# Nine transposes of constants put ahead of three FFN products, and the sum of the second gate moved to the FFN's end

## The chip, the cores and the metric

The kernel runs on one core of a Trainium2 chip. The metric is the device time of one execution in microseconds (us), lower being better; where runs of a kernel differ, their median counts.

## What is computed

One decoder block on a sequence of 256 tokens with 1024 channels, batch 1, in float32:

```python
mod = (jax.nn.silu(c) @ w_ada[l] + b_ada[l]).astype(x.dtype)
sh1, sc1, gt1, sh2, sc2, gt2 = jnp.split(mod[:, None, :], 6, axis=-1)
h = rmsnorm(x, g_mix[l]) * (1.0 + sc1) + sh1
proj = h @ w_in[l]
...
x = x + gt1 * (mixed @ w_out[l])

h = rmsnorm(x, g_ffn[l]) * (1.0 + sc2) + sh2
up = causal_dwconv(h @ w_up[l], ffn_conv_w[l], ffn_conv_b[l])
val, gte = jnp.split(up, 2, axis=-1)
x = x + gt2 * ((jax.nn.silu(gte) * val) @ w_down[l])
```

`w_up` has 2 x 2816 columns and `w_down` 2816 rows, so that the FFN holds most of the work. `gt2`, the second gate, is used only where the FFN's result is added to `x`.

## The kernel before

Channels lie on the 128 partitions and the 256 tokens along the free dimension. Every weight is cut into pieces of 128 x 1024 floats. A piece is loaded by SP's queue into a ring of eight buffers (`raw`, two pieces in a buffer), and split into two tiles of the reduced float32 type of TensorE (PE): `hi`, a rounded copy that ScalarE (ACT) makes at L166, and `lo`, the rest, which VectorE (DVE) makes at L171. The activations are split in the same way (`hhi`, `hlo`; `ahi`, `alo`). A product of 128 x 128 weights with 128 x 256 activations is then three matmuls, `mm3` at L204: hi with hi, hi with the activations' lo, lo with hi. Each loads its own 128 x 128 weights, so that PE runs a chain of pairs of a weight load and a matmul of 256 columns.

The order of every engine's work is the order in which the code is written; no scheduler moves anything. The FFN is a list of 66 steps, `FFN_SEQ`, numbered n from 0: three value and gate pairs ("v", "g") first, and then "d", "v", "g" in turn, "d" being the product with one block of `w_down`. Steps 0 to 2 run together, and the last two in `finish`. A step is 24 matmuls: eight times `mm3`, over the channels for "v" and "g" (into the tiles `pu` and `pg`), over the eight blocks of output channels for "d" (into `pod`). `up_psum` takes the PSUM tile of a step: `pu` from a pool of two banks that other tiles share, `pg` from two banks in turn. After the product of a "v" or "g" step ACT (L758) and DVE (L764) make the convolution out of the PSUM tile.

The second gate is the product of `silu(c)` with one section of `w_ada`. DVE adds it up in `gacc` in eight parts (`gate_part`, L569), at the ends of steps 10, 13 and so on to 31. `gate_rows` (L577) then adds over the partitions with four matmuls of ones, each of 32 by 256 (eight instructions in the trace), into a tile `psg` of the pool of `pu`; `mod_cols` (L600, L608) transposes that on DVE and adds the bias. The first user of the result is `residual` (L695), after the last step but two.

In the first third of the kernel, the attention, PE also transposes probabilities: three transposes of 128 x 128 (`pst`, L503) stand between the two halves of a product (`pb`, `pu` or `pc` there), eight times in all.

Of the kernel before, what the change touches and what calls it, by code (L numbers as in the profile page):

```python
# [14 lines left out]
P = 128  # L15
S = 256
# [34 lines left out]
GROUPS = [(0,), (1,), (2, 3), (4, 5), (6, 7)]  # L51
GATE_STEP = range(1, 9)
ADA_FFN = {(3, i): 10 + 6 * i for i in range(4)}
REP = 16
AHEAD = 2

# [2 lines left out]
def decoder_block(ctx: ExitStack, tc, xT_in, pp, ada1, ada2, wqkv, wst, out):  # L59
# [6 lines left out]
    ACT, DVE, PE, POOL = nc.scalar, nc.vector, nc.tensor, nc.gpsimd  # L66
# [14 lines left out]
    def pw(name):  # L81
        return psw.tile([P, 512], F32, tag="w", name=name)

    def p1(tag, name):
        return ps1.tile([P, 512], F32, tag=tag, name=name)
# [21 lines left out]
    need += [(NS + 2 * c - AHEAD - 0.5, ("w", NS // 2 + c)) for c in range(len(FFN_SEQ) // 2)]  # L107
    need += [(NS + st, ("a2",) + k) for k, st in ADA_FFN.items()]
    order += [k for _, k in sorted(need)]
# [30 lines left out]
    ident = cp.tile([P, P], F32, name="ident")  # L140
    make_identity(nc, ident)
    ones = cp.tile([P, P], F32, name="ones")
# [43 lines left out]
    def hi_to(i):  # L186

        while made["hi"] <= min(i, len(PIECES) - 1):
            k = made["hi"]
            WH[k] = split_hi(piece(k))  # L190
            made["hi"] += 1

    def lo_to(i):

        while made["lo"] <= min(i, len(PIECES) - 1):
            k = made["lo"]
            W[k] = WH[k], split_lo(piece(k), WH[k])
            if k % 2:
                free(("w", k // 2))
            made["lo"] += 1  # L200

    def mm3(o, l, r, start, stop, shared=False, passes=(0, 1, 2)):

        for p in passes:  # L204
            PE.matmul(o, l[p == 2], r[p == 1], start=start and p == 0, stop=stop and p == 2, skip_group_check=shared)  # L205
# [4 lines left out]
    def cut(pair, i, w=P):  # L210
        return tuple(t[:, i * w:(i + 1) * w] for t in pair)


    def add_squares(ss, s2, first, last):

        for t in range(2):
            PE.matmul(ss[:, t * REP:(t + 1) * REP], s2[:, t * P:(t + 1) * P], ones[:, 0:REP], start=(first and t == 0), stop=last,  # L217
                      skip_group_check=True)

    def rms_root(ss, n, name):  # L220
        ms = wk.tile([P, 2], F32, tag="ms", name=f"ms_{name}")
        DVE.tensor_scalar(ms, ss[:, 0:2 * REP].rearrange("p (t n) -> p t n", n=REP)[:, :, 0], 1.0 / n, EPS, op0=OP.mult, op1=OP.add)
        r = wk.tile([P, 2], F32, tag="r", name=f"r_{name}")
# [337 lines left out]
    def gate_part(s, kk):  # L561

        i, k = divmod(kk, 2)
        a = ring["a2", s, i][:, k * D:(k + 1) * D]
        if kk == 0:
            gacc[s] = cp.tile([P, D], F32, tag="gacc", name=f"gacc{s}")
            DVE.tensor_scalar(gacc[s], a, cs[:, 0:1], None, op0=OP.mult)
        else:
            DVE.scalar_tensor_tensor(gacc[s], a, cs[:, kk:kk + 1], gacc[s], op0=OP.mult, op1=OP.add)  # L569
        if k == 1:  # L570
            free(("a2", s, i))
# [3 lines left out]
    def gate_rows(s, ps):  # L575
        for j in range(4):
            PE.matmul(ps[32 * j:32 * j + 32, 0:256], ones[:, 0:32], gacc[s][:, j * 256:(j + 1) * 256],  # L577
                      start=True, stop=True)
        sacc[s] = ps
# [17 lines left out]
    def mod_cols(s):  # L597

        tr = wk.tile([P, 256], F32, tag="tr", name=f"trm{s}")
        DVE.transpose(tr, sacc[s][:, 0:256])  # L600
        v = tr.rearrange("p (k q) -> p k q", q=32)[:, :, 0]
        b = par[:, PC["b_ada"] + 8 * (2 + s):PC["b_ada"] + 8 * (3 + s)]
        if s == 2:
            DVE.tensor_tensor(mod2[:, 0, :], v, bsc1[:, 1, :], op=OP.add)
            DVE.tensor_mul(mod2[:, 0, :], mod2[:, 0, :], par[:, PC["g_ffn"]:PC["g_ffn"] + KT])
        else:
            dst = {0: gate[:, 0, :], 1: mod2[:, 1, :], 3: gate[:, 1, :]}[s]
            DVE.tensor_tensor(dst, v, b, op=OP.add)  # L608
# [18 lines left out]
    for s in range(NS - 2):  # L627

        j, i = divmod(s, 3)
# [117 lines left out]
    PU, Y, ACTV = {}, {}, {}  # L747
    hall = [both(hT, slice(None), kt, slice(None)) for kt in range(KT)]

    def up_psum(n):  # L750
        w, j = FFN_SEQ[n]
        PU[w, j] = pw(f"pu{j}") if w == "v" else p1("vz"[j % 2], f"pg{j}")
        return PU[w, j][:, 0:S]
# [52 lines left out]
    def after_up(n, w, j):  # L806

        after(n + 1, conv_first, w, j, first=True)
        after(n + 1, conv_rest, w, j)
        if w == "g":  # L810
            after(n + 1, act_silu, j)
            after(n + 2, act_mul, j)
            after(n + 3 if j < NJ - 1 else n + 2, act_lo, j)

    def down(n, b, last, ds=None, ps=None):
        j = FFN_SEQ[n][1]
        for d in ds or (2 * b, 2 * b + 1):
            o = pd[b][:, (d % 2) * S:(d % 2 + 1) * S] if ps is None else ps[:, 0:S]
            mm3(o, cut(W[NS + n], d), ACTV[j], (j == 0 and d % 2 == 0) if ps is None else n == nl - 2, last,
                shared=True)  # L820
# [3 lines left out]
    nl = len(FFN_SEQ)  # L824
    for n in range(3, nl):
        w, j = FFN_SEQ[n]
        for f, a in early.pop(n, ()):
            f(*a)
        lo_to(NS + n + AHEAD - 1)
        hi_to(NS + n + AHEAD)  # L830
        for f, a in later.pop(n, ()):
            f(*a)
        if w != "d":
            ps = up_psum(n)
            for kt in range(KT):
                mm3(ps, cut(W[NS + n], kt), hall[kt], kt == 0, kt == KT - 1)
            after_up(n, w, j)
        elif n < nl - 2:
            for b in range(4):
                down(n, b, b == 3 and n == nl - 3)  # L840

        for (_, i), st in ADA_FFN.items():
            if n in (st, st + 3):
                gate_part(3, 2 * i + (n > st))
        end = max(ADA_FFN.values())
        if n == end + 5:
            gate_rows(3, pw("psg3"))
        if n == end + 6:
            mod_cols(3)


# [97 lines left out]
```

## Time and profile before

| | us |
|---|---|
| median of three timed runs | 338.1 |
| the three runs | 334.89, 338.10, 338.63 |
| the profiled execution's own time | 336.0 |
| its span, first to last instruction | 334.2 |

The profile is of one further execution, of which the span leaves out 1.8 us. The times of single instructions come from that execution; the duration of a matmul in it is modelled and overlaps the next one, so that the distance from one matmul's start to the next one's is the number to read.

### The profile page before, as it was taken

How to read it: one execution, taken by the hardware profiler on the slowest of the kernel's cores; microseconds unless marked ns; L12 is line 12 of the kernel's file. 1: busy time of each engine (PE TensorE's matmuls, PEld its weight loads, DVE VectorE, ACT ScalarE, POOL GpSimd, SP SyncE). 2: the span in 40 equal slices, each digit the busy share in tenths (PEclk: the TensorE clock that was granted, in tenths of full speed). 3: DMA queues.
4: the chain of work that ended last, by engine and by line, in shares of the span. 5: the costliest groups of instructions: out<-in, count | busy, mean ns of one | idle time of the engine just before them, and what ended most of it. 6: DMA issues, size and time to landing. Idle time of an engine off the chain costs nothing.

```text
span 334.2 us, 7175 instructions
## 1 busy us (share of the span) xinstructions
PE 325.1 (97%) x2996; PEld 310.1 (93%) x2996; DVE 250.1 (75%) x434; ACT 191.1 (57%) x334; POOL 18.9 (6%) x32
## 2 busy tenths in 40 slices
PE   8999999999999999999999999999999999999992
PEld 8988999888889998899999999999999999999991
DVE  3546774898976897699778888888777777777763
ACT  4334556888873475468655555555455555555460
POOL 1000000010131203000000000000000000000040
PEclk9999999999999999999999999999999999999997
DMA  7999999988996856635567675858464551000003
GB/s 268 419 419 421 411 418 421 358 324 348 358 372 273 310 187 258 227 152 178 202 222 281 218 286 196 297 190 324 151 230 156 224 177 78 0 2 0 2 0 126
DMA packets 12559, 79.23 MB, mean 237 GB/s; under 512 B 1392, under 2 KB 1520, under 8 KB 3952
## 3 DMA queue, kind: packets, MB, share of 16 engines
q1 hardware_dynamic: 12528, 78.79, 61.7%
q8 instruction: 23, 0.38, 0.4%
q14 instruction: 8, 0.07, 0.1%
HBM read 77.74 MB, written 1.05 MB: 236 GB/s over the span
## 4 chain that ended last, share of the span: by engine, by line
issue 56%; PE 33%; DMA 6%; DVE 1%; POOL 1%; SPq 1%; ACT 0%; DVEq 0%
DMA raw<-in_wqkv 6%; PE pox L205 6%; PE pq L205 5%; PE pc L205 4%; PE pb L205 4%; PE pu L205 3%; PE psm L589 2%; PE warm L205 1%; PE pv L205 1%; PE pss L217 1%; PE psr L269 1%; POOL sqr L704 1%; PE pss L471 1%; PE pso L517 1%; PE pst L503 1%
## 5 line engine op out<-in xcount | busy, mean ns | idle before, releaser
L171 DVE TENSOR_TENSOR lo<-raw,hi 128x1024 fp32r<-128x1024 f32 x86 | 104.6, 1222 | 4.9 <-ACT hi L166 4.8
L166 ACT CAST hi<-raw 128x1024 fp32r<-128x1024 f32 x86 | 88.9, 1041 | 2.1 <-PE pox L205 2.1
L205 PE MATMUL pu<-hhi,hi 128*128 128x256 f32 x208 | 58.5, 281 | 0.0
L205 PE MATMUL pu<-hhi,lo 128*128 128x256 f32 x208 | 57.8, 278 | 0.0
L205 PE MATMUL pu<-hlo,hi 128*128 128x256 f32 x208 | 57.7, 278 | 0.0
L205 PE MATMUL pg<-hlo,hi 128*128 128x256 f32 x176 | 49.0, 278 | 0.0
L205 PE MATMUL pg<-hhi,hi 128*128 128x256 f32 x176 | 48.9, 278 | 0.0
L205 PE MATMUL pg<-hhi,lo 128*128 128x256 f32 x176 | 48.9, 278 | 0.0
L205 PE MATMUL pod<-alo,hi 128*128 128x256 f32 x172 | 47.9, 279 | 0.0
L205 PE MATMUL pod<-ahi,lo 128*128 128x256 f32 x172 | 47.7, 278 | 0.0
L205 PE MATMUL pod<-ahi,hi 128*128 128x256 f32 x172 | 47.7, 278 | 0.0
L205 PEld LDWEIGHTS pu<-hhi,hi 128*128 128x128 f32 x208 | 39.1, 188 | 1.4 <-issue 0.7
L205 PEld LDWEIGHTS pu<-hlo,hi 128*128 128x128 f32 x208 | 39.1, 188 | 0.0
L205 PEld LDWEIGHTS pu<-hhi,lo 128*128 128x128 f32 x208 | 39.0, 187 | 0.0
L764 DVE SCALAR_TENSOR_TENSOR fyv<-pu,parf,fyv 128x255 f32<-128x255 f32 (+1 forms) x44 | 21.2, 482 | 20.0 <-ACT fyv L758 19.2
L758 ACT ACTIVATE fyv<-pu,parf 128x256 f32<-128x256 f32 x22 | 12.4, 564 | 39.8 <-PE pu L205 39.8
L205 PEld LDWEIGHTS pg<-hhi,hi 128*128 128x128 f32 x176 | 33.1, 188 | 0.0
L205 PEld LDWEIGHTS pg<-hlo,hi 128*128 128x128 f32 x176 | 33.0, 188 | 0.0
L205 PEld LDWEIGHTS pg<-hhi,lo 128*128 128x128 f32 x176 | 33.0, 187 | 0.0
L205 PEld LDWEIGHTS pod<-alo,hi 128*128 128x128 f32 x172 | 32.3, 188 | 0.1
L205 PEld LDWEIGHTS pod<-ahi,hi 128*128 128x128 f32 x172 | 32.3, 188 | 0.0
L205 PEld LDWEIGHTS pod<-ahi,lo 128*128 128x128 f32 x172 | 32.2, 187 | 0.0
(164 smaller groups left out, 652.2 us busy)
## 6 DMA issues: line engine op xcount, KB each, us to landing
raw<-in_wst SPq DMA_DIRECT2D x43, 1024.0 KB, 4.9
raw<-in_ada SPq DMA_DIRECT2D x24, 1024.0 KB, 8.3
raw<-in_wqkv SPq DMA_DIRECT2D x6, 768.0 KB, 14.6
raw<-in_wqkv SPq DMA_DIRECT2D x4, 256.0 KB, 7.0
out<-xp SPq DMA_DIRECT2D x4, 256.0 KB, 2.8
xp<-in_x SPq DMA_DIRECT2D x3, 256.0 KB, 3.9
raw<-in_wqkv SPq DMA_DIRECT2D x1, 512.0 KB, 9.6
xp<-in_x SPq DMA_DIRECT2D x1, 308.0 KB, 2.7
```

What stands on the lines that cost most here:

```text
L166: ACT.copy(hi[:, 0:n], raw)
L171: DVE.tensor_sub(lo[:, 0:n], raw, hi[:, 0:n].bitcast(F32))
L205: PE.matmul(o, l[p == 2], r[p == 1], start=start and p == 0, stop=stop and p == 2, skip_group_check=shared)
L217: PE.matmul(ss[:, t * REP:(t + 1) * REP], s2[:, t * P:(t + 1) * P], ones[:, 0:REP], start=(first and t == 0), stop=last, skip_group_check= ...
L269: PE.matmul(AR[g][32 * j:32 * j + 32, :], crep[:, k, :], a[:, k % (KT // n), j, :], start=(k == 0), stop=(k == KT - 1))
L471: PE.matmul(AT["s", h][:, c], qT[o:o + DH, p, q], kT[o:o + DH, p, k], start=True, stop=True)
L503: PE.transpose(ps[:, i * P:(i + 1) * P], AT["p", h][0][:, i * P:(i + 1) * P], ident)
L517: PE.matmul(ps[o:o + DH, c], vs[:, i, h * DH:(h + 1) * DH], AT["pt", h][:, k], start=(i == 0), stop=(i == 1))
L589: PE.matmul(sacc[s][32 * j:32 * j + 32, 0:256], crep[:, kk, :], a[:, k, j * 256:(j + 1) * 256], start=(kk == 0), stop=(kk == KT - 1))
L704: POOL.tensor_tensor(s2[:, d, :], s2[:, d, :], s2[:, e, :], op=OP.add)
L758: ACT.activation(Y[w, j], PU[w, j][:, 0:S], AF.Identity, bias=col("ffn_b", f), scale=col("ffn_w", 2 * 2 * NJ + f))
L764: DVE.scalar_tensor_tensor(y[:, d:], ps[:, 0:S - d], col("ffn_w", k * 2 * NJ + f), y[:, d:], op0=OP.mult, op1=OP.add)
```

## The change

Ahead of the products of steps 4, 7 and 10 (`TURNS`; "v" steps all three) PE makes three transposes of the constant tile `ones` into columns 256 to 383 of the step's own PSUM tile, columns that nothing reads. `gate_rows` for the second gate goes from the end of step 33 to the end of step 61, and `mod_cols` from 34 to 62. The eight parts of the sum on DVE stay where they are, as do all loads.

```diff
+TURNS = (4, 7, 10)
...
         if w != "d":
             ps = up_psum(n)
+            if n in TURNS:
+
+                for _ in range(3):
+                    PE.transpose(PU[w, j][:, S:S + P], ones, ident)
             for kt in range(KT):
                 mm3(ps, cut(W[NS + n], kt), hall[kt], kt == 0, kt == KT - 1)
...
-        end = max(ADA_FFN.values())
-        if n == end + 5:
+        if n == nl - 5:
             gate_rows(3, pw("psg3"))
-        if n == end + 6:
+        if n == nl - 4:
             mod_cols(3)
```

PE at the start of step 4 (`pu`), after the last matmuls of step 3 (`pg`); before:

```order
L205 MATMUL pg_1998<-hhi,hi 128x256
L205 MATMUL pg_1998<-hlo,hi 128x256
L205 MATMUL pg_1998<-hhi,lo 128x256
L205 MATMUL pu_2039<-hhi,hi 128x256
L205 MATMUL pu_2039<-hlo,hi 128x256
```

and with the change:

```order
L206 MATMUL pg_1998<-hhi,hi 128x256
L206 MATMUL pg_1998<-hlo,hi 128x256
L206 MATMUL pg_1998<-hhi,lo 128x256
L839 MATMUL pu_2039<-ident,ones 128x128 x3
L206 MATMUL pu_2039<-hhi,hi 128x256
L206 MATMUL pu_2039<-hlo,hi 128x256
```

Three transposes now stand between the two chains of matmuls; the same happens ahead of steps 7 and 10.

PE at the sum of the second gate, which before stands between step 33 (`pod`) and step 34 (`pu`):

```order
L205 MATMUL pod_1979<-ahi_2896,hi 128x256
L205 MATMUL pod_1979<-alo_2930,hi 128x256
L205 MATMUL pod_1979<-ahi_2896,lo 128x256
L577 MATMUL psg_3102<-gacc_2280,ones 32x256 x4
L205 MATMUL pu_3117<-hhi,hi 128x256
```

and with the change between step 61 (`pu`) and step 62 (`pg`):

```order
L206 MATMUL pu_4053<-hhi,hi 128x256
L206 MATMUL pu_4053<-hlo,hi 128x256
L206 MATMUL pu_4053<-hhi,lo 128x256
L578 MATMUL psg_4078<-gacc_2289,ones 32x256 x4
L206 MATMUL pg_4093<-hhi,hi 128x256
```

From step 11 to step 61 nothing but the chain of `mm3` is left on PE.

DVE where the gate's transpose now stands, with the change: behind the convolution of step 61 (`fyv`) and ahead of the `lo` of a later piece; the first user of the gate is in the last row.

```order
L765 SCALAR_TENSOR_TENSOR fyv_4083<-pu_4053,parf,fyv_4083 128x254
L601 STREAM_TRANSPOSE trm_4118<-psg_4078 128x256
L609 TENSOR_TENSOR gate<-trm_4118,xp 128x8
L172 TENSOR_TENSOR lo<-raw,hi 128x1024
L765 SCALAR_TENSOR_TENSOR fyg_4121<-pg_4093,parf,fyg_4121 128x255
L765 SCALAR_TENSOR_TENSOR fyg_4121<-pg_4093,parf,fyg_4121 128x254
L172 TENSOR_TENSOR lo<-raw,hi 128x1024
L774 TENSOR_TENSOR a_4157<-sg_4129,fyv_4083 128x256
L782 TENSOR_TENSOR alo_4161<-a_4157,ahi_4159 128x256
L696 SCALAR_TENSOR_TENSOR xp<-pod_1979,gate,xp 128x256 x2
```

Two instructions came in here, and left their place after step 33.

## Rows read from the trace of the kernel before

**Rows 1.** The page: busy time of PE, and the granted clock in 40 slices.

```profile
PE 325.1 (97%) x2996; PEld 310.1 (93%) x2996; DVE 250.1 (75%) x434; ACT 191.1 (57%) x334; POOL 18.9 (6%) x32
...
PEclk9999999999999999999999999999999999999997
```

**Rows 2.** Chain of waits in order of time, from the FFN's start: start us, us, what.

```profile
135.70 184.61 issue
```

**Rows 3.** Waits of PE in the whole span: us in total, times, longest us.

```profile
PE warm L159 <- POOL mhalf L145: 1.5, 1, 1.5
PE psr L269 <- DMA raw<-in_ada: 0.6, 1, 0.6
PE pss L217 <- POOL sqr L704: 0.5, 2, 0.3
```

**Rows 4.** Windows of nine steps: length, busy PE, PEld, DVE, ACT, POOL, clock, DMA.

```profile
149.24:174.68 25.44, 25.44 (x218) 25.44 (x217) 21.85 (x35) 17.24 (x27) 0.00 (x0) 1.00 0.56 200
...
200.12:225.56 25.44, 25.44 (x218) 25.44 (x217) 21.76 (x31) 14.32 (x22) 0.00 (x0) 1.00 0.62 224
242.97:267.45 24.48, 24.48 (x218) 24.48 (x217) 18.44 (x28) 14.35 (x22) 0.00 (x0) 1.00 0.55 200
...
291.93:316.41 24.48, 24.48 (x218) 24.48 (x217) 18.43 (x28) 13.93 (x21) 0.00 (x0) 1.00 0.01 1
```

**Rows 5.** Timeline of PE around the second gate's sum: start us, us, instruction.

```profile
233.92 0.28 PE L205 MATMUL pod<-ahi,lo 128*128 128x256 f32 x1
234.13 0.64 PE L577 MATMUL psg<-gacc,ones 128*32 128x256 f32 x8
234.70 0.39 PE L205 MATMUL pu<-hhi,hi 128*128 128x256 f32 x1
234.92 0.28 PE L205 MATMUL pu<-hlo,hi 128*128 128x256 f32 x1
235.04 0.28 PE L205 MATMUL pu<-hhi,lo 128*128 128x256 f32 x1
```

**Rows 6.** Chain of waits: twelve matmuls behind a group of three transposes.

```profile
65.32 1.42 PE pb L205 x12
...
69.53 1.37 PE pu L205 x12
```

**Rows 7.** Timeline of PE around one group of three transposes.

```profile
68.92 0.28 PE L205 MATMUL pu<-hhi,lo 128*128 128x256 f32 x1
69.04 0.49 PE L503 MATMUL pst<-ident,pr 128*128 128x128 f32 x3
69.28 0.36 PE L205 MATMUL pu<-hhi,hi 128*128 128x256 f32 x1
69.48 0.28 PE L205 MATMUL pu<-hlo,hi 128*128 128x256 f32 x1
```

**Rows 8.** Timeline of PE behind the first gate's sum: second and twelfth matmul.

```profile
100.25 0.28 PE L205 MATMUL pc<-hlo,hi 128*128 128x256 f32 x1
...
101.43 0.28 PE L205 MATMUL pc<-hhi,lo 128*128 128x256 f32 x1
```

**Rows 9.** Timelines of PE and of DVE: around step 31, and the FFN's end.

```profile
225.80 0.28 PE L205 MATMUL pu<-hhi,lo 128*128 128x256 f32 x1
...
221.64 1.23 DVE L171 TENSOR_TENSOR lo<-raw,hi 128x1024 fp32r<-128x1024 f32 x1
...
225.95 1.28 DVE L569 SCALAR_TENSOR_TENSOR gacc<-raw,cs,gacc 128x1024 f32<-128x1024 f32 x1
...
311.77 1.00 DVE L764 SCALAR_TENSOR_TENSOR fyv<-pu,parf,fyv 128x255 f32<-128x255 f32 x2 [1.39 <-ACT fyv L758]
...
317.81 0.87 DVE L695 SCALAR_TENSOR_TENSOR xp<-pod,gate,xp 128x256 f32<-128x256 f32 x2
```

**Rows 10.** Timeline of DVE: the second gate's transpose and bias.

```profile
234.84 0.45 DVE L600 STREAM_TRANSPOSE trm<-psg 128x256 f32<-128x256 f32 x1 [0.33 <-PE psg L577]
235.32 0.17 DVE L608 TENSOR_TENSOR gate<-trm,xp 128x8 f32<-128x8 f32 x1
```

## Prediction

> **What bounds the kernel now.** I read the page first: PE is busy for 97% of the span, at full granted clock until the last slice [rows 1]. Then the chain of waits in order of time: from 135.70 us on it shows 184.61 us in which nothing that the profile knows of is waited for, up to the norm at the end, 320.3 us [rows 2]. The list of PE's own waits is short, 2.6 us in the whole span, and none of it is in the FFN's steps [rows 3]. So the FFN is bound by the pace at which PE goes through its pairs of weight load and matmul, and a time can change there only through the number of instructions or through that pace.
>
> The pace is therefore the next thing to look at, in windows of nine equal steps, 216 matmuls each (the counts beside them take in one or two at the edges). Two windows ahead of the second gate's sum last 25.44 us, two behind it 24.48 us, at the same granted clock of 1.00 [rows 4]. The edges are starts of steps, chosen so that each window holds nine whole ones. That is 2.827 and 2.720 us a step, or 117.8 and 113.3 ns a matmul, for instructions of the same form. The load on the other engines doesn't explain it: DMA is at 0.55 in a fast window and 0.56 in a slow one. The timeline of PE shows where it turns: at the second gate's sum. Its eight short matmuls start at 234.13, the chain begins again at 234.70, and from its second matmul at 234.92 on the distances are 113 or 114 ns [rows 5]. PE thus has two paces, keeps the one that it has while the chain is unbroken (816 matmuls before, 768 behind, as I count them in the timeline), and takes one anew when the chain begins again after another kind of instruction. The change is about just that: it breaks the chain three times early, and takes away the break at which it turned.
>
> How often does a break end fast? Transposes of the same size stand eight times inside products of the attention. In the chain of waits the twelve matmuls behind three of these groups take 1.37 us, behind the other five 1.42 [rows 6], of which one of each stands there; the shorter ones are at the distance of 113 ns from the second matmul on. Behind breaks of other kinds the chain is nearly always slow: from the second to the twelfth matmul behind the first gate's sum it is 1.18 us in ten distances, 118 ns [rows 8]. The same sum, the second time, ended fast. I take the outcome for a matter of a few nanoseconds at the restart, and so for one that can differ from execution to execution.
>
> **The change part by part.** I sum against the profiled execution, 336.0 us.
>
> The transposes. From the start of the last matmul ahead of a group to that of the second behind it, 68.92 to 69.48, it is 0.56 us [rows 7]; two distances of 0.118 would be 0.235. A group costs 0.325, and three cost +0.98 us. Nothing hides that, since PE is the bound. Nobody else is held up: the products start 0.3 us later, and what feeds and empties them only gains by that. The transposes read constants, and the PSUM bank was already emptied for the product that follows.
>
> The pace from step 10 on. If the last group leaves PE fast, steps 10 to 33, 24 of them, take 0.107 us less each [rows 4]: -2.56. If it was already fast from step 7 or 4, it is 0.32 or 0.64 more; I take the middle, -0.32. If it stays slow, these steps cost nothing more than now, but steps 34 to 61, which are now fast, lose 28 x 0.107 = 3.0.
>
> A faster pace needs its feeding. DVE is the busiest other engine, with 21.76 of 25.44 us while the gate's parts are added up [rows 4]; the same work in 24.48 us would be 89%. The `lo` of step 31 is ready at 222.87, and first read at 225.80 [rows 9], 2.9 us ahead. A window of the FFN with gate parts, run fast, still leaves DVE free for 2.7 us, so I take no wait there. If a wait did come, it would also break the chain and draw a pace anew.
>
> The sum of gate 2. From the last matmul ahead, 233.92, to the second behind, 234.92, it is 1.00 us [rows 5], 0.765 more than two distances, and it costs that at either place. What it does to the pace of the four steps behind it is open: 0 to 4 x 0.107 = 0.43. I take +0.43, since most breaks of other kinds end slow. On DVE the transpose and the bias, 0.45 and 0.17 us [rows 10], now stand behind the convolution that ends at 312.77, and the gate is first used at 317.81 [rows 9]: 4.4 us of room with everything added, so nothing there. The `pl` tiles of the end take the two shared banks after the convolution and this transpose have read them, which is as early. Cover gone, it would cost at most 0.6.
>
> The sum for the fast case: 336.0 + 0.98 - 2.56 - 0.32 + 0.43 = 334.5; between 334.2 (fast from step 4) and 334.9 (from step 10), and 0.4 less where the gate's sum ends fast.
>
> To the timed runs. Three runs of one program at 334.89, 338.10 and 338.63 fit the same idea: an execution that stays slow throughout would be the profiled one plus 32 steps of 0.107, 339.4; two runs lie 0.8 to 1.3 below that, and the third 1.1 below the profiled one. So I read the lowest as a run that turned and the other two as runs that didn't, and the timed executions as 1.1 us shorter than the profile makes them. Then the fast case is 334.5 - 1.1 = 333.4, against a median of 338.1 that is itself of the slow kind. Without that shift it would be 334.5.
>
> [...]
>
> **The rivals.** First: the last group leaves PE slow. For it: five of eight groups in the attention did. Then the chain is slow up to step 61, where before it turned at step 34 in the profiled execution: 336.0 + 0.98 + 3.0 + 0.43 = 340.4, and with the shift 339.3. That is slower than before, by 1.2 us against the median. It decides at the third group alone if each group draws anew, whatever the first two did; if a fast chain stays fast through three transposes, one success in three suffices, with 1 - (5/8)^3 = 0.76 at the rate of [rows 6] against 0.38. No row shows a group that was entered fast; that is the largest unknown.
>
> Second: the pace has nothing to do with the breaks and changed at 234 us for another reason, say a load elsewhere. Against it: the last of DVE's gate parts ends at 227.23 [rows 9], and the chain stayed slow until the sum, 7 us later. Then the transposes are only a cost, 338.1 + 1.0 = 339.1.
>
> [...]
>
> Last, something of the move itself hurts: DVE late, or a break that leaves a worse pattern. More than 3 us of it would be needed.
>
> **How the numbers follow.** A measurement of this kernel tells a change of 1% from none, here 3.4 us, or a time under 334.7. Fast: 0.55, halfway between drawing anew and keeping, 0.38 and 0.76, with 333.4 and a range of its own of 332.9 to 334.9. Slow: 0.33, 339.3. Cost alone: 0.07, 339.1. Worse: 0.05, over 341.5. The fast case is faster by over 1% but for its upper end, so faster gets 0.53, same 0.41, slower 0.06. The range must hold both main cases, 332.9 to 339.5.
>
> **What would show it.** In the changed kernel's trace, windows of nine steps between 11 and 61 should all last 24.48 us; 25.44 is the first rival. Each group of transposes should add 0.32 us, and steps 4 to 10 show which one turned the pace. Behind the gate's sum, four steps tell whether it is lost. PE's waits should be as before. The prediction is wrong if the third group leaves PE slow in most executions, or if a fast chain meets waits on DVE.

## The result, and the profile after

The changed kernel takes 338.98 us, the kernel before 337.62 (medians of 20 runs each): a ratio of 1.0052, with a 95% interval of 1.0029 to 1.0076. It is slower by half a per cent, where 333.4 was forecast; the first rival had 339.3. Three of the 20 runs of the kernel before lie at 334.3 to 335.8 and the others at 337.2 or more; of the changed kernel none lies under 337.57. The times of several kernels here fall into two such groups, and an interval can leave out runs far above a kernel's fastest, so that medians are of all runs and the number of runs in the lower group stands beside them.

The profiled execution took 339.06 us, its span is 337.2. The chain of waits, from the FFN's start (start us, us, what):

```profile
135.41 188.69 issue
324.10 1.48 POOL sqr L705 x2
...
328.39 1.27 PE warm L160 x10
```

The stretch without a wait is 4.08 us longer than in [rows 2]. The list of PE's waits has the same three entries as [rows 3], none in the FFN. So the FFN is again the pace of PE and nothing else. Windows from the first group's start to the second's and on to the third's, then two of nine steps (length, busy PE, PEld, DVE, ACT, POOL, clock, DMA):

```profile
148.96:157.77 8.81, 8.81 (x77) 8.81 (x76) 8.67 (x16) 7.36 (x13) 0.00 (x0) 1.00 0.50 176
157.77:166.58 8.81, 8.81 (x77) 8.81 (x76) 6.46 (x10) 5.11 (x8) 0.00 (x0) 1.00 0.61 227
...
174.80:200.24 25.44, 25.44 (x218) 25.44 (x217) 21.77 (x31) 14.31 (x23) 0.00 (x0) 1.00 0.72 273
...
268.00:293.44 25.44, 25.44 (x219) 25.44 (x218) 18.42 (x28) 14.31 (x22) 0.00 (x0) 1.00 0.23 84
```

The first two hold a group (0.33 us, below) and 72 matmuls at 118 ns each, so they are slow. The last two are 25.44 us long, the slow windows of [rows 4]; the second of them lies where the kernel before, in its profile, had 24.48. All three groups left the chain slow, and it is slow to the end. Around the second group, in the timeline of PE:

```profile
157.65 0.28 PE L206 MATMUL pod<-ahi,lo 128*128 128x256 f32 x1
157.77 0.49 PE L839 MATMUL pu<-ident,ones 128*128 128x128 f32 x3
158.02 0.36 PE L206 MATMUL pu<-hhi,hi 128*128 128x256 f32 x1
158.22 0.28 PE L206 MATMUL pu<-hlo,hi 128*128 128x256 f32 x1
```

It is 0.57 us from the last matmul ahead to the second behind (0.56 in [rows 7]): a group costs 0.33, and three cost 0.99. The sum of gate 2 in its new place:

```profile
313.78 0.28 PE L206 MATMUL pu<-hhi,lo 128*128 128x256 f32 x1
313.99 0.64 PE L578 MATMUL psg<-gacc,ones 128*32 128x256 f32 x8
314.55 0.39 PE L206 MATMUL pg<-hhi,hi 128*128 128x256 f32 x1
314.78 0.28 PE L206 MATMUL pg<-hlo,hi 128*128 128x256 f32 x1
```

That is 1.00 us, as at [rows 5]. On DVE the transpose and the bias stand at 315.61 and 316.08, and the gate is first used at 321.60; nothing waits for them. And the groups of the attention, from the chain of waits:

```profile
65.04 1.42 PE pb L206 x12
...
69.25 1.37 PE pu L206 x12
...
83.73 1.36 PE pu L206 x12
...
87.89 1.36 PE pc L206 x12
```

The three stretches of 1.36 and 1.37 us stand at the same places of eight as in the profile before, of which [rows 6] shows one. That should not be so if each group were a draw.

### The profile page after: what moved, and what is told of

Read it like the earlier page. It is cut to its first block, busy times and chain, and to the rows that moved or that the text cites. A ratio compares the mean times of both kernels' runs of the same rounds, so it can differ in the third digit from the quotient of the medians.

```text
span 337.2 us, 7190 instructions
## 1 busy us (share of the span) xinstructions
PE 327.8 (97%) x3005; PEld 312.7 (93%) x3005; DVE 250.0 (74%) x434; ACT 190.9 (57%) x334; POOL 18.9 (6%) x32
## 4 chain that ended last, share of the span: by engine, by line
issue 56%; PE 34%; DMA 6%; POOL 1%; DVE 1%; SPq 0%; ACT 0%; DVEq 0%
PE pox L206 6%; PE pq L206 6%; DMA raw<-in_ada 6%; PE pc L206 4%; PE pb L206 4%; PE pu L206 3%; PE psm L590 2%; PE warm L206 1%; PE pv L206 1%; PE psr L270 1%; PE pss L218 1%; POOL sqr L705 1%; PE pss L472 1%; PE pso L518 1%; PE pst L504 1%
```

## The experiments

In the texts below a chain of matmuls is fast at 113 and slow at 118 ns; a group is a row of transposes ahead of a product. Transposes and added matmuls write columns that nothing reads. Edits are against the changed kernel unless another is named; a row of dots marks lines left out. Theory A says that what a break leaves is fixed by what stands there, B that moving the sum is what costs, C that every break draws anew.

**The two parts apart.** First the late sum alone, against the kernel before:

```diff
-        end = max(ADA_FFN.values())
-        if n == end + 5:
+        if n == nl - 5:
...
-        if n == end + 6:
+        if n == nl - 4:
```

> The sum of gate 2 at step 61, no transposes. Theory A (what ends a break slow or fast is fixed by what stands there, the transposes end slow, and most executions of the kernel before never turned at its sum either): about the kernel before's usual time, 337.6, and 1.0 us under the changed kernel's 338.98; all FFN steps up to 61 at 2.827 us. Theory B (the kernel before usually turns fast at step 33, and moving the sum is what costs): 28 x 0.107 = 3.0 us over the kernel before, and about the changed kernel's time or more.

337.84 us in 10 runs (337.25 to 339.60), against 336.86 before: ratio 1.004, interval 1.0003 to 1.0078. The chain is slow from the FFN's start to step 61. The lower group is gone: 9 of the 19 runs before in this comparison lie under 335.5, none of these does. Its distance to the changed kernel, 1.14 between the medians of two comparisons, is near the 0.99 of three groups. Then the transposes alone:

```diff
-        if n == nl - 5:
+        end = max(ADA_FFN.values())
+        if n == end + 5:
...
-        if n == nl - 4:
+        if n == end + 6:
```

> The three groups of transposes, the sum of gate 2 at step 33 as before. Theory A: 1.0 us over the kernel before in the usual execution, 338.6; the steps behind each group at 2.827 us; behind the sum fast in few executions, so that the profile probably shows slow ones there. Theory B: fast behind the sum, 1.0 us over the kernel before and 3 us under the changed kernel.

338.11 us (334.61 to 340.35, four of ten under 336.5), ratio 1.0017, 0.9966 to 1.0068. In the profile the first group left the chain fast and the second made it slow again, in windows of 72 matmuls each:

```profile
149.60:157.85 8.25, 8.25 (x75) 8.25 (x74) 8.14 (x15) 6.81 (x12) 0.00 (x0) 1.00 0.52 180
158.09:166.66 8.57, 8.57 (x75) 8.57 (x74) 6.53 (x10) 5.18 (x8) 0.00 (x0) 1.00 0.57 224
```

A group can thus undo the one before it. The lower times are back with the sum at 33, while with the same three groups and the late sum none of 20 runs had them. So the sum at 33 leaves a fast chain in some executions, and B holds in part: the late sum takes away a chance, not a rule.

**What a break may be.** Other numbers of transposes, and one matmul of the chain's own type:

```diff
-TURNS = (4, 7, 10)
+COUNTS = (1, 2, 3, 4, 5, 6, 8)
...
-            if n in TURNS:
-
-                for _ in range(3):
+            for _ in range(COUNTS[(n // 3 * 2 - (w == "v")) % 7] if 4 <= n < nl - 4 else 0):
```

> The changed kernel with 1, 2, 3, 4, 5, 6 or 8 transposes ahead of every v and g product of steps 4 to 61, 38 breaks, each number five or six times. Theory A: each number, at one kind of place, ends the same way each time; if three end slow, others may end fast, and a number that does shows 24 distances of 113 ns per step behind it. Theory C (each break draws anew, at the 3 of 8 of the attention): some 14 of 38 end fast, spread over all numbers. Time by the number of transposes alone, 156 at 0.108: some 17 us over the changed kernel, less what fast stretches give.

354.29 us in one run. Of 39 groups 6 were entered fast, and all six ended slow. Six transposes ended fast four times of four when entered slow; three, once of six; five, once of six; one, two, four and eight never. The second kernel has one matmul there, of a varied number of columns:

```diff
-TURNS = (4, 7, 10)
+COLS = (32, 64, 96, 128, 160, 192, 224)
...
+            if 4 <= n < nl - 4:
+                c = COLS[(n // 3 * 2 - (w == "v")) % 7]
+                PE.matmul(PU[w, j][:, S:S + c], W[NS + n][0][:, 0:P], hall[0][0][:, 0:c], start=True, stop=True)
```

> The changed kernel with one more matmul of the chain's own type, of 32, 64, 96, 128, 160, 192 or 224 columns in place of the transposes, ahead of every v and g product of steps 4 to 61. It shifts the start of the next weight load against the matmul by one short distance. Theory A: a number of columns always ends the same way; those that end fast stay so up to the next break. If the pace were bound to breaks by another kind of instruction, nothing changes: all slow, 38 x 0.12 = 4.5 us over the kernel before. Theory C: fast and slow in no order.

341.82 us in one run; all 39 were entered slow and ended slow. But the seven numbers of columns were one and the same test. From the added matmul to the second one behind it, with 224 columns and with 32:

```profile
169.26 0.27 PE L838 MATMUL pg<-hhi,hi 128*128 128x224 f32 x1
...
169.49 0.28 PE L206 MATMUL pg<-hlo,hi 128*128 128x256 f32 x1
...
175.03 0.18 PE L838 MATMUL pu<-hhi,hi 128*128 128x32 f32 x1
...
175.25 0.28 PE L206 MATMUL pu<-hlo,hi 128*128 128x256 f32 x1
```

It is 0.23 and 0.22 us: the weight loads stand 0.11 and 0.12 us apart there with every number of columns, and the matmuls behind follow them. A shift by the number of columns did not come about, so this run does not tell whether one would turn the pace. It shows that one more pair of the chain's own kind did not, in 39 cases.

**Six transposes, or one group.** First one group of six:

```diff
-TURNS = (4, 7, 10)
+TURNS = (4,)
...
-                for _ in range(3):
+                for _ in range(6):
```

> Six transposes ahead of step 4 alone, the sum of gate 2 at step 61. In the run with seven numbers, six transposes entered slow ended fast four times of four, three ended fast once of six, and every group entered fast ended slow. Theory A (the number fixes the end): fast from step 4 to 61, 337.84 + 0.65 - 58 x 0.107 = 332.3, the profile with 2.72 us a step. Theory C (drawn anew): 332.3 in some executions, 338.5 in most, median 338.5.

339.15 us, one of ten at 331.85, before 337.79. So six transposes do not end fast by their number: theory A in this form falls. Chains that are entered at the same slow pace can leave the same group differently; whatever differs between them I call the phase of the chain, and no view here shows it. The one at 331.85 is where 332.3 was expected.

Then one group of three (only the first of the two edits):

> Three transposes ahead of step 4 alone, the sum of gate 2 at step 61: the changed kernel without its second and third group. If three transposes always end slow here: 337.84 + 0.33 = 338.2, 0.65 under the changed kernel. If they end fast in part of the executions (as in one of the two profiles so far) and the later groups undo that: times of two kinds, 332.0 and 338.2, which the changed kernel doesn't have.

338.83 us, one of ten at 333.51, where 332.0 was expected of a fast one.

Three groups of six (only the second):

> The changed kernel with six transposes in each group. If a group turns slow into fast and fast into slow: fast in steps 4 to 6, slow in 7 to 9, fast from 10 to 61, 337.84 + 1.95 - 55 x 0.107 = 333.9. If a fast chain stays fast: 333.6 and steps 7 to 9 at 2.72 us in the profile. If drawn anew: about 339.5.

335.91 us, five of ten at 333.6 to 335.1, two at 336.7 and 336.9 and three at 339.4 to 339.7; in the profiled one, of the last three, no group ended fast.

One group of six, and the sum back at step 33:

```diff
-        if n == nl - 5:
+        if n == 33:
...
-        if n == nl - 4:
+        if n == 34:
```

> Six transposes ahead of step 4 alone, the sum of gate 2 at step 33 as in the kernel before. It shows what the sum does to a fast chain. If it ends slow: fast in steps 4 to 33 alone, 337.84 + 0.65 - 30 x 0.107 = 335.3. If the chain stays fast: 332.3, and where the sum stands doesn't matter.

336.69 us, five of ten at 334.7 to 335.7; in the profile the group and the sum ended slow, so that it told nothing on a fast chain.

**A group ahead of each of twenty products.** Three transposes each:

```diff
-TURNS = (4, 7, 10)
+TURNS = range(4, 62, 3)
```

> The change's own group, three transposes, ahead of all twenty v products of steps 4 to 61, the sum of gate 2 at step 61. Theory C' (a slow chain ends fast behind a group in some 1 of 5, a fast one always ends slow): two to four fast stretches, each ended by the next group. If a fast chain could stay fast, fast stretches would run on over several groups. Time: 17 groups more than the changed kernel, 17 x 0.325 = 5.5, less 0.32 a fast stretch: about 344.

342.21 us in one run. From one group's start to the next one's, in windows:

```profile
149.20:158.01 8.81, 8.81 (x78) 8.81 (x76) 8.67 (x16) 7.36 (x13) 0.00 (x0) 1.00 0.52 187
158.01:166.51 8.50, 8.50 (x78) 8.50 (x77) 6.35 (x10) 5.01 (x8) 0.00 (x0) 1.00 0.57 228
166.51:175.32 8.81, 8.81 (x77) 8.81 (x76) 6.83 (x11) 4.87 (x8) 0.00 (x0) 1.00 0.46 170
175.32:183.82 8.50, 8.50 (x78) 8.50 (x76) 7.15 (x11) 4.67 (x8) 0.00 (x0) 1.00 0.82 304
183.82:192.63 8.81, 8.81 (x77) 8.81 (x76) 7.37 (x11) 4.87 (x8) 0.00 (x0) 1.00 0.53 184
192.63:201.44 8.81, 8.81 (x77) 8.81 (x76) 7.25 (x11) 4.78 (x8) 0.00 (x0) 1.00 0.76 298
201.44:209.94 8.50, 8.50 (x77) 8.50 (x76) 7.16 (x11) 4.67 (x8) 0.00 (x0) 1.00 0.52 179
209.94:218.75 8.81, 8.81 (x78) 8.81 (x77) 7.36 (x11) 4.88 (x8) 0.00 (x0) 1.00 0.82 311
```

A window of 8.50 is fast. The ends are slow, fast, slow, fast, slow, and from there slow, fast, slow in turn to the last group. So regular an order is no draw at each group, and theory C falls with it for this execution. It would fit a group that leads from one phase of the chain to the next, of which one is fast; the phases themselves are not seen. Groups of five and six in turn:

```diff
-TURNS = (4, 7, 10)
+TURNS = {"v": 5, "g": 6}
...
-            if n in TURNS:
-
-                for _ in range(3):
+            if 4 <= n < nl - 4:
+                for _ in range(TURNS[w]):
```

> Five transposes ahead of every v product and six ahead of every g product, steps 4 to 61. In the run with seven numbers a group of six that followed one of five ended fast four times of five, the fifth time because five had already ended fast. If five always leads into a phase from which six ends fast, the stretches behind the groups of six are fast (two steps of three). If the phase is drawn by the execution, as the single group of six showed, mostly slow. Time: 213 transposes at 0.109, some 23 us over 337.84, less 0.21 for each fast stretch.

360.60 us in one run, with a cycle of four groups from the fifth on, of which one ended fast. The pair alone, once:

```diff
-TURNS = (4, 7, 10)
+TURNS = {4: 5, 5: 6}
...
-                for _ in range(3):
+                for _ in range(TURNS[n]):
```

> Five transposes ahead of step 4 and six ahead of step 5, the sum of gate 2 at step 61. If the pair turns: 337.84 + 1.2 - 57 x 0.107 = 332.9 in most executions. If it is drawn: times of two kinds, 332.9 and 339.0, as many fast ones as two draws of 1 in 4 give, and the first lost again by the second group.

339.27 us, none of ten under 338.3: ratio 1.0043, 1.0019 to 1.0067. In the profile five left the chain fast, and six made it slow.

**The number of groups.** The expectations rest on a cycle of three from the start (theory D). Two groups:

```diff
-TURNS = (4, 7, 10)
+TURNS = (4, 7)
```

> The changed kernel with two groups of three, ahead of steps 4 and 7. In the run with twenty groups of three the ends came in a cycle from the fifth group on, fast, slow, slow: each group moves the chain on by one of three phases, of which one is fast. Theory D: a chain starts in a slow phase, most often the one two groups ahead of fast (one group alone ended fast in 1 execution of 10, three in none of 20, since three are a full turn). Then two groups end fast in most executions: 337.84 + 0.65 - 55 x 0.107 = 332.6, and the profile is fast from step 7 to 61. Theory C' (each group draws anew from a slow chain): fast in 2 of 10, median 338.5.

333.04 us, all of four runs at 332.68 to 333.17: ratio 0.9864, interval 0.9798 to 0.9929. Windows of three steps behind the first and the second group, and of nine steps:

```profile
149.44:157.92 8.48, 8.48 (x74) 8.48 (x73) 8.37 (x15) 7.03 (x13) 0.00 (x0) 1.00 0.52 172
158.16:166.32 8.16, 8.16 (x75) 8.16 (x74) 6.02 (x10) 4.68 (x8) 0.00 (x0) 1.00 0.62 231
174.48:198.96 24.48, 24.48 (x219) 24.48 (x218) 21.79 (x31) 14.35 (x22) 0.00 (x0) 1.00 0.76 282
...
280.56:305.04 24.48, 24.48 (x219) 24.48 (x218) 18.43 (x28) 14.34 (x22) 0.00 (x0) 1.00 0.01 1
```

The second group turns the chain, and no third one turns it back: it is fast for 1320 matmuls, up to the sum, which leaves it slow. DVE is as busy as in the slow windows, and PE doesn't wait for it in these steps.

Four groups, `TURNS = (4, 7, 10, 13)`:

> Four groups, ahead of steps 4, 7, 10 and 13. Theory D: four are one full turn and one group, and end as one alone: slow in most executions, 337.84 + 1.3 - 0.3 = 338.8, a fast one in ten at 333.9. Theory C': fast in 2 of 10 likewise, so that this run tells the two apart only with the others.

333.98 us, all of four runs at 333.28 to 334.24: ratio 0.989, 0.9834 to 0.9946. Theory D had slow here and is wrong on this.

Five, `TURNS = (4, 7, 10, 13, 16)`:

> Five groups, ahead of steps 4, 7, 10, 13 and 16. Theory D: they end as two do, fast in most executions: steps 7 to 9 and 16 to 61 fast, 337.84 + 1.63 - 49 x 0.107 = 334.2. Theory C': fast in 2 of 10, median 339.2.

338.99 us, none of ten under 337.2: ratio 1.0062, 1.0022 to 1.0102. D is wrong here too. By the times, what the last group leaves agrees with the first five ends of the run with twenty groups: one group slow (nine of ten), two fast (four of four), three slow (20 of 20), four fast (four of four), five slow (ten of ten). But the groups ahead of the last are in no fixed order. With five groups, from one group's start to the next one's:

```profile
148.89:157.39 8.50, 8.50 (x78) 8.50 (x77) 8.36 (x16) 7.06 (x12) 0.00 (x0) 1.00 0.55 182
157.39:166.20 8.81, 8.81 (x78) 8.81 (x76) 6.77 (x10) 5.41 (x9) 0.00 (x0) 1.00 0.61 229
166.20:175.01 8.81, 8.81 (x78) 8.81 (x76) 6.71 (x11) 4.77 (x8) 0.00 (x0) 1.00 0.53 168
175.01:183.51 8.50, 8.50 (x78) 8.50 (x76) 7.16 (x11) 4.68 (x8) 0.00 (x0) 1.00 0.82 317
```

That is fast, slow, slow, fast, and then slow. The first three ends are fast, slow, slow also in the run with the transposes alone; slow, fast, slow with four and with twenty groups; and slow three times in the changed kernel. Only the third is the same in all five profiles, and it is slow.

**Distance, and the sum's place.** First `TURNS = (4, 5)`:

> Two groups of three one step apart, ahead of steps 4 and 5. If only the number of groups counts: as two groups at 4 and 7, two steps of 0.107 sooner fast, 333.04 - 0.2 = 332.8. If the length of the chain between the groups counts too (24 matmuls in place of 72), or that the second stands ahead of a g product: slow, 338.5.

338.04 us, three of ten at 332.3 to 333.6; ratio 0.998, 0.9907 to 1.0052. The profiled one is of these three. So the number of groups alone doesn't decide; the chain between the groups, or the product behind the second, may count as well.

Then `TURNS = (4, 7)` with the sum back at step 33, by the edit shown above:

> Two groups of three ahead of steps 4 and 7, the sum of gate 2 at step 33 as in the kernel before: what the move of the sum is worth. In all three profiles in which the sum met a fast chain it left it slow. If so: fast from 7 to 33 alone, 333.04 + 28 x 0.107 = 336.0. If a chain can stay fast behind the sum: 333.0.

336.59 us, eight of ten at 335.4 to 337.0; ratio 1.0019, 0.9974 to 1.0064. Windows of nine steps ahead of the sum and behind it:

```profile
207.85:232.33 24.48, 24.48 (x219) 24.48 (x218) 21.78 (x31) 14.35 (x22) 0.00 (x0) 1.00 0.75 276
242.50:267.94 25.44, 25.44 (x219) 25.44 (x218) 18.40 (x28) 14.31 (x22) 0.00 (x0) 1.00 0.50 185
```

In this profile the sum makes a fast chain slow. Between the medians of two comparisons the early sum costs 3.55 us, where 3.0 was worked out. That is what the late sum is worth once the chain is fast.

## Why the prediction was wrong

**The bound and its two paces** were right: PE's pace was what moved, and the changed kernel's FFN shows no wait. The windows of two groups show both paces at the lengths that the prediction had.

**The step that failed** is the chance of the fast case, 0.55, "halfway between drawing anew and keeping". Neither happens. Over all profiles 27 groups were entered fast, and all 27 ended slow; so nothing is kept. And the last group is not a draw with three chances in eight: a third group of three transposes, at step 10, left the chain slow in all five profiles that have one, and none of the 20 runs of the changed kernel lies under 337.57. Three of eight was a count of places, not a rate: in the attention the ends at seven of the eight places were the same in all 18 profiles, which one profile could not show. The largest unknown had been named, but given two answers of which both were wrong.

That the third group is to blame is shown by leaving it out: two groups were fast in four runs of four, three in none of 20. Why the third ends slow is shown only where the second has made the chain fast, by the 27 of 27. In the profile of the changed kernel all three groups were entered slow and left slow; slow chains left a group fast in 32 cases of 100 over all profiles, and what decides among them stays open.

**A chain keeps its pace** only while nothing holds it up, and that was misread. Of the 768 matmuls behind the sum, which the prediction took as one fast chain, the last 35 run at 118 ns. At the start of the FFN's last step PE waited for a tile of DVE:

```profile
317.46 0.43 DVE L781 TENSOR_TENSOR alo<-a,ahi 128x256 fp32r<-128x256 f32 x1 [0.47 <-ACT ahi L775]
...
317.77 0.28 PE L205 MATMUL pod<-ahi,hi 128*128 128x256 f32 x1
317.95 0.39 PE L205 MATMUL pod<-alo,hi 128*128 128x256 f32 x1
318.17 0.28 PE L205 MATMUL pod<-ahi,lo 128*128 128x256 f32 x1
318.29 0.28 PE L205 MATMUL pod<-ahi,hi 128*128 128x256 f32 x1
```

The tile is ready at 317.89 and its first reader starts at 317.95; ahead of it the distances are 113 ns, behind it 118, and no instruction of another kind stands there. The same happens at this place in the profiles of the late sum alone and of the pair of five and six, and in that of three groups of six early in the FFN, behind a delay of 0.09 us. In all four cases a fast chain went on slow. So a delay in the chain makes it slow as a group does; that it would draw a pace anew is not shown.

**The sum** of the first rival comes out near the result, 339.3 against 338.98, in part by luck. Its groups were sized at 0.98 and measured 0.99, or 1.14 between two kernels. The FFN's stretch was to grow by 4.41 (0.98, 3.0 and 0.43) and grew by 4.08. The difference is the 0.43 for the four steps behind the gate's sum: there the changed kernel lost 0.10, since in the profile before only two and a half of these steps were fast, and the wait above cost 0.17. Another 1 us by which the profiled execution stayed under the 340.4 lies elsewhere: 0.29 ahead of the FFN, and 0.8 in the last norm, where the matmuls of `keep_clock` took 1.27 us and not 2.30: the granted clock over them was 0.50 in the profile before, and 0.90 here. The shift of 1.1 us from the profile to the timed runs is not found: the profiled execution of the changed kernel took 339.06, and its median is 338.98. It happened to stand where these other differences were.

**The place of the sum.** That its outcome is open was right: entered slow it ended fast in 3 of 13 profiles, entered fast it ended slow in all of 5. The reading of the three timed runs was right in kind, too: in six comparisons 3 of 20, 9 of 19, 3 of 31, none of 13, 4 of 13 and 8 of 18 runs of the kernel before lie under 336, and I take these for executions that turn at the sum, as the profiled one did. So 28 fast steps were counted as lost that most executions never had. Against the usual execution the change loses its transposes, and against all of them a chance of 3 us as well: medians 337.62 and 338.98.

**Open** stays what the phases are, why the third group ends slow when it is entered slow, and why groups at 4 and 5 end otherwise than at 4 and 7. The kernel with two groups was found by trying; nothing here predicts the ends for another chain.

## What to carry to other kernels

Where PE is the bound, compare the distance between its matmuls over stretches of equal instructions, also between executions: one profile of a kernel with two paces may be of the rarer kind, and its timed runs then fall into two groups. If a break turns the pace, keep the one that does so and remove every break and every delay behind it; a second copy for safety can undo the first. Here two groups in place of three, with the late sum, took 1.4% off the kernel before, in four runs.

## What the runs showed of the hardware

The same chain of weight loads and matmuls of 128 x 256, at a granted clock of 1.00 (2.4 GHz), ran at 117.8 or at 113.3 ns a matmul for hundreds of matmuls. In the FFN it became fast only behind a break by instructions of another kind (32 of 100 groups and 3 of 13 sums entered slow, and once the matmuls ahead of the FFN), and slow behind every break (27 groups, 5 sums) and every delay (4, the shortest of 0.09 us) that it met while fast. One more matmul of the chain's own type never changed it in 39 cases, all slow, and took the same time with 32 columns as with 224: 0.22 and 0.23 us to the second matmul behind. Three transposes of 128 x 128 cost 0.33 us in the chain; the eight instructions of the gate's sum, of 32 by 256, cost 0.77.
